# A one-core decoder layer in float32: where the state-space tables, the bias rows, the first far row and the first down weights stand in the queues

## The chip, the cores and the metric

The kernel runs on one core of one Trainium2 chip. The metric is the device time of one execution, in microseconds (us), the median of several runs. "PE" is the matrix engine (TensorE), "DVE" VectorE, "ACT" ScalarE, "POOL" GpSimd, "SP" SyncE, which here does nothing but issue DMAs. ACT and POOL can issue DMAs as well. Every engine works through its own instructions strictly in the order in which they stand in its queue; where one waits, all behind it wait.

## The reference, cut to what matters

One layer, 2048 tokens, width 1024, everything in float32:

```python
h = rms_norm(x, norm1_g); proj = h @ w_in
o_a = swa_sink_mixer(...)        # near attention, window 128, 4 heads
o_b = s5_mixer(...)              # state-space part: A_bar = exp(A*dt), a scan over all tokens, GELU, GLU
o_c = nsa_mixer(...)             # far attention: compressed, selected and window branch, 4 heads
mixed = concat(rms_norm(o_a), rms_norm(o_b), rms_norm(o_c))
x = x + mixed @ w_out
h2 = rms_norm(x, norm2_g)
x = x + relu(h2 @ w_up)**2 @ w_down     # hidden width 4096
```

Both attentions add a bias by distance, looked up in a table `rel_bias` of 32 rows and 8 heads.

## The kernel before

Every float32 product is made of three matmuls on split words (`wh`/`wl`, `hh`/`hl`: the upper bits and the rest), so each operand is cast on ACT (`wh`) and subtracted on DVE (`wl`). The work runs in five stages.

**Front (0 to 153 us here).** The projection is made in tiles of 128 tokens. First the state-space input `u`, then eight tiles `pm_a` of the near heads' columns, then sixteen of `pm_b` and `pm_c`. A tile's product is 24 matmuls into a PSUM bank, of which there are two for `pm`; ACT scales it out of the bank into `po` (L190), squares it into `sq` (L192, one buffer), DVE sums the squares into the last columns of `po` (L193), and POOL stores `po` (L194). A token row's scale `rx` needs the sum of squares of its `x` row. Rows 8 to 15 are loaded in `row_sum`: POOL copies one element of the newest `po_a` sum into the buffer (L118), so that the load, issued by POOL behind it (L119), cannot start earlier; ACT then squares the row (L120). Meanwhile DVE makes the tables of the state-space part (`ssm_tables`): exponentials `rho` of 0 to 16 times the log of the decay, sines and cosines of 11 doubled angles, power tables `k_Ea`/`k_Eb`, and products with the inputs B and C. The bias rows are made in `bias_vectors`: a table `tab` and one-hot matrices `boh` are loaded, PE multiplies them (`bpr`, L797), ACT copies the result to `brv`, POOL stores it (`r`). Their pool "bv" reuses the tables' memory. Weights are loaded into a ring `wraw` (`wr_a`, `wr_b`, `wr_c`) by SP. The order of this stage is a scheduler's: code order with raised priorities (`W_HOIST`).

**Second half of the front, the scan, near attention (153 to 555 us).** Not touched.

**Far attention (555 to 1200 us).** `phase_mix` runs a planner: tasks yield an engine, a cost in ns and a closure, are ranked, and are placed by the planner's own clock; its order is then fixed by hand (`manual_schedule`). The far rows are 16 blocks of 128 tokens. A row loads `tc` (queries, keys, values), POOL scales them (`qdc`, L865), PE turns them (`ptqc`, L872), three branches of logits follow (`pqc`, `pqw`, `pqs`), with their maxima `nmc`, `nmw`, `nms` on DVE; results `ot` are added on POOL into `oc`. A finished row is joined with `oa`, `ob` in `mix`, scaled by row factors (`r_a`, `r_b`, `nr`), turned (`ptx`) and multiplied by `w_out`, whose raw rows `oraw` are split into `wo_h` (ACT) and `wo_l` (DVE, L1491). `early_norms` and `row_norms` make the row factors with a chain of small operations on POOL (L51 to L61). `kBs` holds a mask, loaded as `ohr` and cast (L1412). The GLU of the state-space part (`gpm`, `ga` L767, `ob`) fills PE until about 604 us.

**Up (1200 to 1802 us)** and **Down (1802 us to the end)**: products of 2x2 blocks by seven multiplications, named "1675243" in this order. In Down a chunk `c` of 512 hidden channels needs seven weights `dw`, made from the raw chunk `dr` by differences `dt` on POOL (L2662), a cast on ACT (L2228) and a subtraction on DVE (L2229). Code hoisted by `DOWN_HOIST` places the first chunk's weights among the last instructions of Up, where `e` and `ex` (L2491) free PE's banks `pub`, `puc`. Products "1" and "6" go through `acc…u` on ACT and POOL, the others are added on DVE (`acc`, L2715).

Of the kernel before, what the change touches and what calls it, by code (L numbers as in the profile page):

```python
# [93 lines left out]
def phase_front(tc, C, x, norm1_g, w_in, uT, pd, rh_a, prm, ssm_d, rx_d, consts, extra, later, x_t, r_last, last_bank):  # L94

    nc = tc.nc
    with ExitStack() as ctx:
# [78 lines left out]
        open_, box_x, w_more = {}, [], []  # L176

        def product(t, hs, w, kind, c0, n, part=None):
# [17 lines left out]
            if (kind, t // 8) == ("a", 0):  # L196
                row_sum(t + 8, o[:, n:n + 1])
# [10 lines left out]
        for half in range(2):  # L208
# [25 lines left out]
            with tc.tile_pool(name=f"a_psu{half}", bufs=1, space=PSUM, reuse_waits="tile") as ps_u:  # L234
# [30 lines left out]
                if half == 0:  # L265
# [5 lines left out]
                    gen = ssm_tables(tc, C, S, kp, kf, prm, ssm_d["k"])  # L271
# [85 lines left out]
def ssm_tables(tc, C, S, pool, first, prm, dkp):  # L357
# [22 lines left out]
    with ExitStack() as ctx2:  # L380
        tp2 = ctx2.enter_context(tc.tile_pool(name="si2", bufs=1))
        with ExitStack() as ctx:
# [11 lines left out]
            jt = C["ramp"]  # L394
            xr = tmp([P, 17, G], "xr")
# [12 lines left out]
            sincos(nc, k, sc, th)  # L408

# [38 lines left out]
            yield  # L448
            for dst, top, low in ((C1, c_re, c_im), (C2, c_im, c_re)):
                nc.sync.dma_start(dst[0:64], top)  # L450
                nc.sync.dma_start(dst[64:128], low)
            B1, B2 = (tp2.tile([P, G, 16], F32, name="t_" + n) for n in ("B1", "B2"))
            nc.sync.dma_start(B1[0:64], b_re)
            nc.sync.dma_start(B1[64:128], b_im)
            nc.sync.dma_start(B2[0:64], b_im)
            nc.sync.dma_start(B2[64:128], b_re)
            dT = tp2.tile([16, G], F32, name="t_dT")
            nc.sync.dma_start(dT, d_skip[0].rearrange("(g q) -> q g", q=16))
# [326 lines left out]
def bias_vectors(tc, tp, ps, rel_bias, oh2, ohs, r2, rs):  # L785
# [4 lines left out]
    nc.sync.dma_start(tab[0:32], rel_bias)  # L790
    for src, dst, n in ((oh2, r2, 432), (ohs, rs, 384)):
        for j in range(src.shape[1] // n):
            sl = slice(n * j, n * j + n)
            o = tp.tile([33, 432], F32, tag="b_oh", name=f"boh{n}{j}")
            nc.sync.dma_start(o[:, 0:n], src[:, sl])
            pr = ps.tile([P, 512], F32, tag="pt", name=f"bpr{n}{j}")
            nc.tensor.matmul(pr[0:8, 0:n], tab, o[:, 0:n], start=True, stop=True)  # L797
# [575 lines left out]
def phase_mix(tc, flow, ctx, C, x, gains, B, cmp, w_out, out_norm_g, g2, pd, oa_d, ob, x1, hT, xs, rr, rh, ss_a, ss_b, oc_d, gated_all, release, over, up):  # L1373
# [3 lines left out]
    if True:  # L1377
# [32 lines left out]
        ohr = lp.tile([P, L], F32, tag="sl", name="ohr", bufs=4)  # L1410
        nc.sync.dma_start(ohr[64:96], C["blk"])
        nc.vector.tensor_copy(kBs[64:96], ohr[64:96])  # L1412
# [10 lines left out]
        rows_there, norms_there, most = Event(), Event(), Event()  # L1423
# [42 lines left out]
        def opening():  # L1466
# [87 lines left out]
        def keys(i, tq, twice_k):  # L1554
# [17 lines left out]
            fire(ev["k"], t)  # L1572
# [338 lines left out]
        def finished(i):  # L1911
# [15 lines left out]
            else:  # L1927
                box["oc"] = ev["oc"]
            yield landing(t, 5e5)
            mix = box["mix"]  # L1930
            def rest():
                yield rows_there
                yield norms_there
                for c, r, ns in ((slice(0, 256), late["ra"], 474), (slice(256, 768), late["rb"], 700)):
                    yield "POOL", ns, lambda: nc.gpsimd.tensor_scalar(mix[:, c], mix[:, c], r[:, i:i + 1], 1.0, op0=ALU.mult, op1=ALU.mult)

            def third():
# [5 lines left out]
                yield "POOL", RSQRT_NS, lambda: rsqrt_into(nc, late["sm"], r, ss, 1.0 / 256, 1, "nq", nc.gpsimd)  # L1943
                t = yield "POOL", 474, lambda: nc.gpsimd.tensor_scalar(dst, src, r, 1.0, op0=ALU.mult, op1=ALU.mult)
# [182 lines left out]
        spawn(early_norms(), 60, t0)  # L2127
        spawn(opening(), 60, t0)
# [473 lines left out]
def phase_down(tc, x1, w_down, vd, out):  # L2602
# [8 lines left out]
    with ExitStack() as ctx:  # L2611
# [309 lines left out]
def _shape_constants():  # L2921
# [12 lines left out]
    for off in (29, 30):  # L2934
# [5 lines left out]
        "k_ramp": np.tile(np.arange(T16 + 1, dtype=f), (P, 1)),  # L2940
# [41 lines left out]
```

## Time and profile before

| | |
|---|---|
| median of 3 runs | 2422.76 us (2421.95, 2422.76, 2429.80) |
| the profiled execution | 2422.61 us, its span 2420.8 us, mean granted clock 0.992 |
| PE busy | 2360.3 us, 97% of the span |
| DVE, ACT, POOL busy | 1782.6, 1294.4, 1087.2 us |

PE's row is the one to read: 60.5 us of the span are without a matmul. The profile's list of waits names for each engine and line who ended its idle time, and a table of stretches gives the clock that was granted to PE. A row of the timeline is start, duration, engine, line, operation, result and operands, and in brackets the idle time before it and who ended it.

### The profile page before, as it was taken

To read this page: it belongs to the slowest core of one execution; us is meant where nothing else is said; L and a number is where in the kernel's file an instruction comes from. 1 tells how busy PE (TensorE), PEld (TensorE's weight loads), DVE (VectorE), ACT (ScalarE), POOL (GpSimd) and SP (SyncE) were. 2 spreads that over 40 slices of the span, in tenths; PEclk is the share of its full clock that TensorE was granted. 3 is DMA by queue.
4 is the path that set the end of the run, shared out by engine and by line. 5 is a ranking of instruction groups with operands and counts; after the bars stand their busy time and mean duration, and the time that the engine had idled before them with its cause. 6 is when DMAs were issued, how large, how long until landed. Compare 5 with 4: busy or idle time off the path is not lost. (4 is left out here: it accounts for less than half of the span.)

```text
span 2420.8 us, 37163 instructions
## 1 busy us (share of the span) xinstructions
PE 2360.3 (97%) x12292; PEld 2019.6 (83%) x12292; DVE 1782.6 (74%) x3470; ACT 1294.4 (53%) x2726; POOL 1087.2 (45%) x1210
## 2 busy tenths in 40 slices
PE   8899999999899999999999999999999999999999
PEld 7798999787788889888788888888877888888887
DVE  7866885885877888886855557545567888888886
ACT  5443545775777676665655555544454344433442
POOL 1331122323443454332676665566562554545547
PEclk9899999999999999999999999999999999999999
DMA  8674554641322343112666677655548444344435
GB/s 269 179 253 140 179 157 144 168 151 53 129 75 79 92 120 118 43 56 96 196 205 195 195 217 215 191 158 147 148 145 272 135 130 123 100 138 133 128 102 197
DMA packets 409766, 361.60 MB, mean 149 GB/s; under 512 B 45132, under 2 KB 360290, under 8 KB 407492
## 3 DMA queue, kind: packets, MB, share of 16 engines
q1 hardware_dynamic: 355460, 295.83, 40.5%
q10 hardware_dynamic: 43296, 34.09, 4.5%
q0 software_dynamic: 10816, 29.31, 3.6%
q8 instruction: 97, 1.59, 0.3%
q14 instruction: 97, 0.79, 0.1%
HBM read 236.31 MB, written 128.02 MB: 150 GB/s over the span
## 5 line engine op out<-in xcount | busy, mean ns | idle before, releaser
L2228 ACT CAST v<-vr 128x512 fp32r<-128x512 f32 x224 | 139.4, 624 | 295.7 <-DMA vr<-vd 139.7
L2229 DVE TENSOR_TENSOR v<-vr,v 128x512 fp32r<-128x512 f32 x224 | 237.9, 1071 | 80.2 <-ACT v L2228 79.2
L2392 DVE TENSOR_TENSOR ul<-fs,uh 128x512 fp32r<-128x512 f32 x124 | 112.2, 923 | 104.7 <-ACT uh L2391 104.5
L2694 PE MATMUL pdc<-dw,v 128*128 128x512 f32 x768 | 184.9, 389 | 2.6 <-DVE acc L2715 2.6
L2694 PE MATMUL pda<-dw,v 128*128 128x512 f32 x768 | 184.8, 389 | 0.7 <-ACT acc0u L2700 0.7
L2694 PE MATMUL pdb<-dw,v 128*128 128x512 f32 x768 | 184.8, 389 | 0.0
L2694 PEld LDWEIGHTS pdc<-dw,v 128*128 128x128 f32 x768 | 144.0, 188 | 33.3 <-DVE acc L2715 3.4
L2694 PEld LDWEIGHTS pda<-dw,v 128*128 128x128 f32 x768 | 144.1, 188 | 31.0 <-ACT acc0u L2700 1.1
L2694 PEld LDWEIGHTS pdb<-dw,v 128*128 128x128 f32 x768 | 144.1, 188 | 30.3 <-DVE acc L2715 0.4
L2391 ACT CAST uh<-fs 128x512 fp32r<-128x512 f32 x124 | 74.3, 620 | 160.0 <-POOL fs L2380 123.2
L2392 DVE TENSOR_TENSOR ul<-ur,uh 128x512 fp32r<-128x512 f32 x93 | 87.9, 948 | 68.5 <-ACT uh L2391 68.5
L2539 POOL TENSOR_TENSOR ev<-ex,e 128x512 f32<-128x512 f32 x32 | 43.1, 1347 | 206.7 <-ACT ex L2522 206.7
L1662 ACT CAST ths<-pps 128x512 fp32r<-128x512 f32 (+1 forms) x144 | 79.0, 564 | 72.2 <-PE pps L1646 63.2
L2522 ACT ACTIVATE e<-e 128x512 f32<-128x512 f32 x128 | 81.0, 633 | 53.4 <-DVE e L2491 51.4
L1667 DVE TENSOR_TENSOR tls<-pps,ths 128x512 fp32r<-128x512 f32 (+1 forms) x144 | 92.6, 657 | 23.0 <-ACT ths L1662 22.2
L1997 PE MATMUL pw<-wo_h,mh 128*128 128x512 f32 x256 | 106.6, 416 | 1.2 <-DVE mx L2019 0.9
L2470 PE MATMUL pub<-fh,uh 128*128 128x512 f32 x256 | 101.7, 397 | 4.9 <-DVE e L2491 4.9
L1997 PE MATMUL pw<-wo_h,ml 128*128 128x512 f32 x256 | 104.6, 409 | 0.0
L1997 PE MATMUL pw<-wo_l,mh 128*128 128x512 f32 x256 | 104.2, 407 | 0.0
L2470 PE MATMUL puc<-fl,uh 128*128 128x512 f32 x256 | 99.8, 390 | 1.6 <-DVE fl L2410 1.5
L2470 PE MATMUL pub<-fh,ul 128*128 128x512 f32 x256 | 100.6, 393 | 0.0
L2470 PE MATMUL puc<-fh,ul 128*128 128x512 f32 x256 | 99.8, 390 | 0.7 <-DVE ul L2392 0.7
(581 smaller groups left out, 7604.0 us busy)
## 6 DMA issues: line engine op xcount, KB each, us to landing
vr<-vd SPq DMA_DIRECT2D x224, 256.0 KB
ur<-in_w_up SPq DMA_DIRECT2D x124, 256.0 KB
vd<-ev SPq DMA_DIRECT2D x96, 256.0 KB
vd<-e ACTq DMA_DIRECT2D x64, 256.0 KB
dr<-in_w_down SPq DMA_DIRECT2D x32, 512.0 KB
mx<-in_x ACTq DMA_DIRECT2D x32, 256.0 KB
x<-mx ACTq DMA_DIRECT2D x32, 256.0 KB
vd<-e SPq DMA_DIRECT2D x32, 256.0 KB
```

The costliest lines, as they stand in the source:

```text
L1662: yield "ACT", cast_ns(n), lambda: nc.scalar.copy(th[:, 0:nb], pt[:, 0:nb])
L1667: t = yield "DVE", sub_ns(n), lambda: nc.vector.tensor_tensor(tl[:, 0:nb], pt[:, 0:nb], th[:, 0:nb], op=ALU.subtract)
L1997: t = yield "PE", mm_ns(512), lambda: nc.tensor.matmul(pw[n], a[half][:, j], b[k][:, sl], start=k == 0 and m == 0, stop=k == NK - 1 and m ...
L2228: nc.scalar.copy(dh, src)
L2229: nc.vector.tensor_tensor(dl, src, dh, op=ALU.subtract)
L2391: yield "ACT", 621, lambda: self.nc.scalar.copy(h, src.tile)
L2392: t = yield "DVE", 900, lambda: self.nc.vector.tensor_tensor(l, src.tile, h, op=ALU.subtract)
L2470: nc.tensor.matmul(banks[b], w[:, j], h[:, j], start=k < 4 and j == 0 and i == 0, stop=j == HALF - 1 and i == 2, skip_group_check=True)
L2522: t = yield "ACT", 640, lambda: nc.scalar.activation(r, r, func)
L2539: t = yield "POOL", 1400, lambda: nc.gpsimd.tensor_tensor(E["v" + q].tile, E[x].tile, E[y].tile, op=op)
L2694: nc.tensor.matmul(bank[b, q], x[:, q, j], y[:, j], start=first and j == 0 and n == 0, stop=j == 1 and n == 2, skip_group_check=True)
```

## The change

Four edits in one.

1. **Tables.** The angles are made first; the 17 exponentials are no longer evaluated as one 128x544 polynomial but as one exponential of 128x32 and four doubling products. B, C and D of the tables, `tab` and the one-hot matrices `boh` are loaded by POOL instead of SP; the former wait for the square of row 7, the one-hot matrices have six buffers instead of one.
2. **Weights of `pm_b`.** Each `wr_b` load waits for a POOL copy out of the newest `po_a` sum.
3. **First far rows.** The mask's load and cast become a ranked task (`marks`); the last row's factors (`row_norms`) and the first far row's factors and scalings go to DVE; the loads of `w_out` wait until the first row's `mix` loads are asked for.
4. **Down.** Of the first chunk's weights only "7" and "5" keep a place in the pool that is free early; "2", "4", "3" go to the pool behind it, each with a buffer of its own.

```diff
 def fetch_w(half, kind, c0, n, k, pool, bufs, eng):
     raw = pool.tile([P, n], F32, tag="wraw", ...)
+    if (kind, half) == ("b", 0):
+        nc.gpsimd.tensor_copy(raw[:, 0:1], newest[0])
...
 # product()
     if (kind, t // 8) == ("a", 0):
-        row_sum(t + 8, o[:, n:n + 1])
+        newest[:] = [o[:, n:n + 1]]
+        row_sum(t + 8, newest[0])
...
 # ssm_tables()
-    nc.vector.tensor_tensor(xr, adr.unsqueeze(1).broadcast_to([P, 17, G]), jt.unsqueeze(2)..., op=ALU.mult)
-    rho = exp_acc(nc, tp, xr, [P, 17, G], "e2")
-    nc.vector.tensor_copy(rho16, rho[:, 16])
     for j in range(11):
         nc.vector.tensor_scalar(th[:, j], adi, float(2 ** j), None, op0=ALU.mult)
     sincos(nc, k, sc, th)
+    rho = tmp([P, 17, G], "rho")
+    e = exp_acc(nc, tp, adr, [P, G], "e2")
+    nc.vector.memset(rho[:, 0], 1.0)
+    nc.vector.tensor_copy(rho[:, 1], e)
+    for n in (1, 2, 4, 8):
+        nc.vector.tensor_tensor(rho[:, n + 1:2 * n + 1], rho[:, 1:n + 1], rho[:, n:n + 1].broadcast_to([P, n, G]), op=ALU.mult)
+    nc.vector.tensor_copy(rho16, rho[:, 16])
...
+    for dst in (C1, C2, B1, B2):
+        nc.gpsimd.tensor_copy(dst[:, 0, 0:1], seen)
-    nc.sync.dma_start(dst[0:64], top)
+    nc.gpsimd.dma_start(dst[0:64], top)
...
 # bias_vectors()
-    nc.sync.dma_start(tab[0:32], rel_bias)
+    nc.gpsimd.dma_start(tab[0:32], rel_bias)
-    o = tp.tile([33, 432], F32, tag="b_oh", name=f"boh{n}{j}")
-    nc.sync.dma_start(o[:, 0:n], src[:, sl])
+    o = tp.tile([33, 432], F32, tag="b_oh", name=f"boh{n}{j}", bufs=6)
+    nc.gpsimd.dma_start(o[:, 0:n], src[:, sl])
...
 # phase_mix: far attention
-    ohr = lp.tile([P, L], F32, tag="sl", name="ohr", bufs=4)
-    nc.sync.dma_start(ohr[64:96], C["blk"])
-    nc.vector.tensor_copy(kBs[64:96], ohr[64:96])
+    def marks():
+        yield R["sl"]
+        ohr = lp.tile([P, L], F32, tag="sl", name="ohr", bufs=4)
+        t = yield "SP", 60, lambda: nc.sync.dma_start(ohr[64:96], C["blk"])
+        yield landing(t, 3e5)
+        t = yield "DVE", 1220, lambda: nc.vector.tensor_copy(kBs[64:96], ohr[64:96])
...
 def norms():
     yield most
-    t = yield "POOL", 3300, row_norms
+    t = yield "POOL", 250, lambda: nc.gpsimd.tensor_copy(late["ra"], r_ae)
+    fire(norms_there, t)
+    t = yield "DVE", 1500, row_norms
...
 # finished(i)
+    engine, e = ("POOL", nc.gpsimd) if i else ("DVE", nc.vector)
-    yield "POOL", ns, lambda: nc.gpsimd.tensor_scalar(mix[:, c], mix[:, c], r[:, i:i + 1], ...)
+    yield engine, ns, lambda: e.tensor_scalar(mix[:, c], mix[:, c], r[:, i:i + 1], ...)
...
 # phase_down()
-    for o in ORDER[2:6]:
+    for o in ORDER[2:4]:
         w_high.tile([P, 2, 2, N], F32R, tag="w" + o, name="dw" + o)
+    for o in ORDER[4:]:
+        w_last.tile([P, 2, 2, N], F32R, tag="w" + o, name="dw" + o)
```

The order on the engines moves at three places that matter below (a row is line, operation, result and operands, shape; the changed kernel's lines are numbered some 2 to 25 higher).

ACT in the front, before: from the fourth `wh_b` to the third eviction of `pm_a`; `x_746` is row 8.

```order
L154 ACTIVATE wh_b_3_939<-wr_b_3_936,g_109 128x384
L349 ACT_TABLE_LOAD
L349 ACTIVATE k_sc<-k_sc 128x704
L154 ACTIVATE wh_b_4_1036<-wr_b_4_1033,g_109 128x384
L190 ACTIVATE po_a<-pm_a_716,rx 128x384
L154 ACTIVATE wh_b_5_1043<-wr_b_5_1040,g_109 128x384
L192 ACTIVATE sq_a<-po_a 128x384
L154 ACTIVATE wh_b_6_1085<-wr_b_6_1082,g_109 128x384
L190 ACTIVATE po_a<-pm_a_798,rx 128x384
L192 ACTIVATE sq_a<-po_a 128x384
L120 ACTIVATE x_746,ss<-x_746 128x1024
L190 ACTIVATE po_a<-pm_a_892,rx 128x384
```

The same place now (`x_749` is row 8):

```order
L192 ACTIVATE po_a<-pm_a_719,rx 128x384
L194 ACTIVATE sq_a<-po_a 128x384
L192 ACTIVATE po_a<-pm_a_801,rx 128x384
L194 ACTIVATE sq_a<-po_a 128x384
L120 ACTIVATE x_749,ss<-x_749 128x1024
L192 ACTIVATE po_a<-pm_a_901,rx 128x384
L156 ACTIVATE wh_b_0_877<-wr_b_0_873,g_109 128x384
L156 ACTIVATE wh_b_1_885<-wr_b_1_881,g_109 128x384
L194 ACTIVATE sq_a<-po_a 128x384
L120 ACTIVATE x_832,ss<-x_832 128x1024
L192 ACTIVATE po_a<-pm_a_957,rx 128x384
```

All `wh_b` and the table load have left the stretch ahead of the first two evictions; row 8 still stands ahead of the third, and row 9 with two `wh_b` ahead of the fourth.

DVE from Up to Down, before: `dw…<-dr` and `dw…<-dt` are the weights "7", "5", "2", "4" in this order.

```order
L2491 TENSOR_TENSOR e_20951<-puc_20932,ex_20913 128x512
L2229 TENSOR_TENSOR dw_21152<-dt_21129,dw_21152 128x1024
L2229 TENSOR_TENSOR dw_21160<-dt_21125,dw_21160 128x1024
L2229 TENSOR_TENSOR dw_21168<-dr_21120,dw_21168 128x1024
L2229 TENSOR_TENSOR dw_21173<-dt_21171,dw_21173 128x1024
L2491 TENSOR_TENSOR e_20951<-pub_20952,e_20951 128x512
L2519 TENSOR_TENSOR e_20983<-e_20983 128x512
```

The same place now:

```order
L2514 TENSOR_TENSOR e_20966<-puc_20947,ex_20928 128x512
L2252 TENSOR_TENSOR dw_21168<-dt_21145,dw_21168 128x1024
L2252 TENSOR_TENSOR dw_21176<-dt_21141,dw_21176 128x1024
L2514 TENSOR_TENSOR e_20966<-pub_20967,e_20966 128x512
L2542 TENSOR_TENSOR e_20998<-e_20998 128x512
```

The weights "2" and "4" now stand 10 rows further on, behind six `v` of the first products and right ahead of weight "3"; on ACT their casts moved likewise, behind both `de` and ahead of the copies `acc0u`, `acc1u`.

DVE at about 606 us, shortly before the third far row is turned, before:

```order
L1568 SCALAR_TENSOR_TENSOR kAw<-ptkc_7161,gains,kAw 64x128
L1570 COPY kBw<-kAw 64x128
L1571 COPY kBs<-kAs 64x128
L1720 TENSOR_TENSOR otw_7279<-ptow_7247,ww 128x512
L1598 ISA slw_7257,nmw<-pqw_7259,b_sel 128x384
```

Now the ten steps of `row_norms` (eight of 128x1, then two) stand between `kAw` and `kBw`; the last two of them and what follows:

```order
L1461 TENSOR_SCALAR r_ce<-r_ce 128x16
L1463 TENSOR_TENSOR r_sel<-r_sel,r_ce 128x128
L1588 COPY kBw<-kAw 64x128
L1589 COPY kBs<-kAs 64x128
L1740 TENSOR_TENSOR otw_7269<-ptow_7246,ww 128x512
```

More of the change, by code (lines that the diff above doesn't have):

```diff
@@ L354, with ssm_tables @@
 WEIGHTS_AT = 2
-def ssm_tables(tc, C, S, pool, first, prm, dkp):
+def ssm_tables(tc, C, S, pool, first, prm, dkp, seen):
     nc = tc.nc
@@ L448, in ssm_tables @@
             yield
+            B1, B2 = (tp2.tile([P, G, 16], F32, name="t_" + n) for n in ("B1", "B2"))
+            for dst in (C1, C2, B1, B2):
+                nc.gpsimd.tensor_copy(dst[:, 0, 0:1], seen)
             for dst, top, low in ((C1, c_re, c_im), (C2, c_im, c_re)):
-                nc.sync.dma_start(dst[0:64], top)
[L451 to L456, printed above, removed]
+                nc.gpsimd.dma_start(dst[0:64], top)
+                nc.gpsimd.dma_start(dst[64:128], low)
+            nc.gpsimd.dma_start(B1[0:64], b_re)
+            nc.gpsimd.dma_start(B1[64:128], b_im)
+            nc.gpsimd.dma_start(B2[0:64], b_im)
+            nc.gpsimd.dma_start(B2[64:128], b_re)
             dT = tp2.tile([16, G], F32, name="t_dT")
-            nc.sync.dma_start(dT, d_skip[0].rearrange("(g q) -> q g", q=16))
+            nc.gpsimd.dma_start(dT, d_skip[0].rearrange("(g q) -> q g", q=16))
             zz = tp2.tile([16, 112], F32, name="t_zz")
@@ L1422, in phase_mix @@
         wout = {(k, n): Event() for k in range(NK) for n in range(2)}
-        rows_there, norms_there, most = Event(), Event(), Event()
+        rows_there, norms_there, most, asked, marked = (Event() for _ in range(5))
         pm = kp.tile([P, P], F32, name="pm")
@@ L1472, in opening @@
             fire(opened, t)
+            yield asked
             for n in range(2):
@@ L1475, in opening @@
                 for k in range(NK):
+                    if (k, n) == (2, 0):
+                        later = Event()
+                        fire(later, t + 1500)
+                        yield later
                     yield R["xt"]
@@ L1571, in keys @@
             t = yield "DVE", 300, lambda: nc.vector.tensor_copy(kBs[0:64, ks], kAs[0:64, ks])
-            fire(ev["k"], t)
+            if not i:
+                yield marked
+            fire(ev["k"], max(t, marked.time))
         def values(i):
@@ L1928, in finished @@
                 box["oc"] = ev["oc"]
+                fire(asked, t)
+            engine, e = ("POOL", nc.gpsimd) if i else ("DVE", nc.vector)
             yield landing(t, 5e5)
@@ L1934, in rest @@
                 for c, r, ns in ((slice(0, 256), late["ra"], 474), (slice(256, 768), late["rb"], 700)):
-                    yield "POOL", ns, lambda: nc.gpsimd.tensor_scalar(mix[:, c], mix[:, c], r[:, i:i + 1], 1.0, op0=ALU.mult, op1=ALU.mult)
+                    yield engine, ns, lambda: e.tensor_scalar(mix[:, c], mix[:, c], r[:, i:i + 1], 1.0, op0=ALU.mult, op1=ALU.mult)
             def third():
@@ L2775, in consts @@
             nc.sync.dma_start(C["ident"], k_ident)
-            for n, src in (("ramp", k_ramp), ("forced", k_forced), ("rows31", k_rows31)):
+            for n, src in (("forced", k_forced), ("rows31", k_rows31)):
                 C[n] = cp.tile(list(src.shape), F32, name="c_" + n)
```

35 lines of the change are left out of this document (16 added, 19 removed).

## The prediction, made before the changed kernel was run

> **What bounds the kernel.** I read the page's first part, then the list of waits of PE, then the timeline around each long wait and the table of stretches for the granted clock.
>
> ```profile
> PE 2360.3 (97%) x12292; PEld 2019.6 (83%) x12292; DVE 1782.6 (74%) x3470; ACT 1294.4 (53%) x2726; POOL 1087.2 (45%) x1210
> ...
> PE bpr L797 <- DMA boh<-in_k_oh: 6.6, 2, 5.3
> PE pub L2470 <- DVE e L2491: 4.9, 2, 4.7
> ```
>
> PE is busy all but 60.5 us, and the change takes no matmul away. So it can only shorten PE's waits and the slow clock behind them. A wait row gives total, count and longest: the bias product and the last `pub` lead. All four edits stand beside such a wait, and each is summed where it stands.
>
> **Front: what is lost now.** Rows of the timeline, then the table of stretches (PE, PEld, DVE, ACT, POOL busy; granted clock; DMA).
>
> ```profile
> 61.62 0.61 ACT L154 ACTIVATE wh_b<-wr_b,g 128x384 fp32r<-128x384 f32 x1 [5.84 <-DMA wr_b<-in_w_in]
> 65.36 0.69 PE L83 MATMUL pm_a<-wh_a,hh 128*128 128x384 f32 x1 [3.31 <-ACT po_a L190]
> 67.72 0.19 POOL L118 COPY x<-po_a 128x1 f32<-128x1 f32 x1 [12.09 <-DVE po_a L193]
> 74.32 1.06 ACT L120 ACTIVATE x<-x 128x1024 f32<-128x1024 f32 x1 [5.11 <-DMA x<-in_x]
> 96.06 0.34 SPq L790 DMA_DIRECT2D tab<-in_rel_bias  x1
> 98.69 1.59 PE L797 MATMUL bpr<-boh,tab 33*8 33x432 f32 x2 [5.34 <-DMA boh<-in_k_oh]
> 114.05 0.88 PE L797 MATMUL bpr<-boh,tab 33*8 33x432 f32 x2 [1.27 <-DMA boh<-in_k_oh]
> 153.27 0.53 PE L83 MATMUL pm_c<-wh_c,hh 128*128 128x396 f32 x1
> ```
> ```profile
> 66.00:67.00 1.00, 1.00 (x5) 1.00 (x4) 0.97 (x5) 1.00 (x3) 0.00 (x0) 0.50 0.10 24
> 71.00:72.00 1.00, 1.00 (x7) 1.00 (x6) 0.96 (x3) 0.00 (x0) 0.48 (x1) 0.99 0.77 223
> 104.00:105.00 1.00, 1.00 (x5) 0.88 (x3) 1.00 (x3) 0.00 (x0) 1.00 (x1) 0.50 0.59 218
> 116.00:117.00 1.00, 1.00 (x5) 1.00 (x4) 0.88 (x5) 0.00 (x0) 0.39 (x1) 0.50 0.39 134
> ```
>
> ACT stands 5.84 on a weight of `pm_b`, the eviction behind it comes late, PE waits 3.31, and the clock is 0.50 until about 71. The one-hot loads cost 5.34 and 1.27, each with a slow stretch behind it. At half clock half of the time is lost: of the slow stretches, 65.4 to 71.1, 98.7 to 105.1 and 115.3 to 118.6 (read off the same table, of which the first and last rows of each kind stand above), 2.8, 3.2 and 1.65. With the waits, 9.92, that is 17.5 us.
>
> *What the change removes.* The `wh_b` casts leave ACT's queue ahead of those evictions: the 3.31 goes. The exponentials shrink:
>
> ```profile
> L321 DVE TENSOR_TENSOR e2t<-e2p,e2r 128x544 f32<-128x544 f32 x6 | 4.4, 726 | 0.2
> L322 DVE TENSOR_SCALAR e2p<-e2t 128x544 f32<-128x544 f32 x6 | 2.6, 441 | 0.1
> L316 DVE SCALAR_TENSOR_TENSOR e2r<-e2k,e2xc 128x544 f32<-128x544 f32 x1 | 0.7, 726 | 0.0
> ...
> L326 DVE TENSOR_SCALAR e2t<-t_xr 128x544 f32<-128x544 f32 x1 | 0.4, 434 | 0.0
> ...
> L155 DVE SCALAR_TENSOR_TENSOR wl_b<-wr_b,g,wh_b 128x384 fp32r<-128x384 f32 x8 | 4.9, 615 | 0.1
> L193 DVE TENSOR_REDUCE po_a<-sq_a 128x6 f32<-128x384 f32 x6 | 3.3, 549 | 2.1 <-ACT sq_a L192 2.1
> ```
>
> Twelve rows take 7.0, eleven more of 0.43 to 0.73 sum to 6.8. The 23 small ones that replace them cost about 0.19 each (the smallest rows of DVE, 0.17, stand below), 4.4, and the doublings 1.1: 8.3 saved. The eight `wl_b` (4.9), four sums (2.2) and some 3.6 of DVE's idle time leave the stretch too, so the table's memory is free about 19 earlier: `tab` is asked for near 77 instead of 96, the one-hots land near 83 to 84.
>
> *What it adds.* Row 8's load still waits for the sum of the first `po_a` (67.72 above). DVE, still in order, reaches that sum near 66.8, one earlier than now; the square of row 8 then runs near 72.5 instead of 74.32, and it stands ahead of the third eviction. PE, no longer stalled for the third tile, is ready for the fifth at 70.45 and waits until 74.2: 3.8 plus 2.8 slow. So the 3.31 comes back two tiles later. The bias products now stand between the fifth and seventh tiles (81 to 93), three tiles earlier, and catch their data later than PE wants it: 2.3, and 1.5 slow; one `brv` buffer makes them wait for each other, 1.1; row sums that now stand behind DVE's table, 2.7. After: 3.8+2.8+2.3+1.5+1.1+2.7 = 14.2 against 17.5, −3.3. Walking the new order instance by instance with these durations, PE reaches the first `pm_c` at 145.4 to 148.9 where it now stands at 153.27; some of the row sums' cost then still lies ahead, and from this view I get −4.4. I take **−5**, a little beyond both, since the 2.7 is the least certain of the new waits. Its ends are −10 (half of the 14.2 absent) and +3 (the table no earlier than 90, so that the bias products cost 6.6 and 4.85 slow as now, in place of 2.3, 1.5 and 1.1). POOL's new loads and copies are costed at nothing: POOL stood idle for 12.09 before 67.72 and works on small things there; what it costs if that cover is gone is rival C. The `wr_b` gate itself makes no one wait: `pm_b` is wanted after eight tiles of `pm_a`, and eight casts of 0.61 fit between their evictions.
>
> **Mask gate at 558.**
>
> ```profile
> 559.25 1.22 DVE L1412 CAST kBs<-ohr 32x2048 fp32r<-32x2048 f32 x1 [5.34 <-DMA ohr<-in_k_blk]
> 559.25 1.30 POOL L59 TENSOR_TENSOR r_t<-r_t,r_h 128x16 f32<-128x16 f32 x1
> 561.33 0.47 PE L83 MATMUL gpm<-glu_h,zh 128*128 128x512 f32 x1 [2.26 <-DVE ga L767]
> 562.72 1.68 POOL L865 TENSOR_TENSOR qdc<-tc,rh_c 128x512 f32<-128x512 f32 x2
> 563.87 1.11 PE L872 MATMUL ptqc<-c_ident,qdc 128*128 128x128 f32 x4 [0.52 <-POOL qdc L865]
> 564.00:565.00 1.00, 1.00 (x5) 1.00 (x6) 0.00 (x0) 0.00 (x0) 0.39 (x1) 0.50 0.01 4
> ```
>
> Without the cast `ga` comes early and the 2.26 goes. But PE's next need, `qdc`, stands on POOL behind a chain of tiny operations that ends at 562.7 with or without the cast (one of them took 1.30 beside it). PE then waits there: **−0.5**, ends −2.8 (both waits gone) and 0. The cast's 1.22 moves behind `ga`, and the first reader of the mask, the selected branch, comes later than that; its 5.34 of idle time shows that DVE has room.
>
> **Far opening near 606.**
>
> ```profile
> 605.02 1.82 SPq L1478 DMA_DIRECT2D oraw<-in_w_out  x4
> 607.88 0.38 SPq L1517 DMA_DIRECT2D tc<-pb  x1
> 612.79 2.60 POOL L865 TENSOR_TENSOR qdc<-tc,rh_c 128x512 f32<-128x512 f32 x2 [1.70 <-DMA tc<-pb]
> 614.41 1.12 PE L872 MATMUL ptqc<-c_ident,qdc 128*128 128x128 f32 x4 [3.60 <-POOL qdc L865]
> 117.01 0.17 DVE L60 TENSOR_SCALAR rqt<-rqt 128x8 f32<-128x8 f32 x1
> ```
>
> PE's 3.60 ends with a load, `tc`, that SP issues behind four `oraw`. Now two `mix` loads go first, of which one waits until `ob` is stored; `oraw` and `tc` follow. So `tc` is no earlier: the edit relieves POOL, which wasn't last. DVE gets ten factor steps of about 0.2 ahead of `kBw`, 2.1 us, and eight steps and three scalings, 2.5 us, ahead of the first row's next softmax, where it is nearly full. The two blocks together, 4.6, delay what DVE feeds to PE (`kBw`, then the split exponentials); my walk of the new order puts PE 3 later by 625. POOL gives up the same steps, in its own slower form, and a queue that is shorter there brings later `qdc` earlier. I take **+1**: the walk, less 2 for that. Ends: −3 (`tc` lands earlier, most of the 3.60 gone) and +5 (both DVE blocks in full).
>
> **Down.**
>
> ```profile
> 1787.70 4.40 DVE L2229 TENSOR_TENSOR dw<-dt,dw 128x1024 fp32r<-128x1024 f32 x2
> 1792.02 3.37 DVE L2229 TENSOR_TENSOR dw<-dr,dw 128x1024 fp32r<-128x1024 f32 x1
> 1796.56 0.68 DVE L2491 TENSOR_TENSOR e<-pub,e 128x512 f32<-128x512 f32 x1
> 1797.30 0.80 PE L2470 MATMUL pub<-fh,uh 128*128 128x512 f32 x1 [4.72 <-DVE e L2491]
> 1801.56 1.65 ACT L2228 CAST v<-vr 128x512 fp32r<-128x512 f32 x3
> 1813.91 3.02 PE L2694 MATMUL pda<-dw,v 128*128 128x512 f32 x12 [0.71 <-ACT acc0u L2700]
> 1819.00 1.66 PE L2694 MATMUL pdc<-dw,v 128*128 128x512 f32 x6 [2.07 <-DVE acc L2715]
> ```
>
> Weights "2" and "4" hold DVE from 1792.02 to 1796.56, in front of the `e` that frees PE's bank. They move 10 rows on, so `e` runs at about 1792.0: 4.5 earlier, and with it the 4.72 goes and the slow clock behind (1797.3 to 1801.3, 2.0). Now 4.72+2.0+0.71+2.07 = 9.5 are lost up to "4". But who is late next? PE wants the first `v` near 1798.2, and their casts on ACT (1801.56 now) come 3.4 earlier only: 1.3. `acc0u`, which empties a bank, now stands on ACT behind the casts of "2", "4" and "3", each of 1.1 by the row of `v` (three of half the size take 1.65): PE finds it 2.3 late. The sums `acc`, 4.5 earlier, are still 1.7 late, since PE comes earlier too. That is 5.3 of new waits: 9.5 − 5.3 = 4.2. Read the other way, the row at 1819.00 ends with DVE's `acc`, whose chain starts at `e` and moves by 4.5. I take **−4.5**; ends −7 (half of the new waits) and −1.5 (half as much again).
>
> **Sum.** −5 −0.5 +1 −4.5 = −9 on the profiled 2422.61 (span 2420.8 and 1.8 around it, equal to the median 2422.76 within 0.2): 2413.6. All low ends together make −23, all high ends +6.5. A change under 0.3%, 7.3 us, can hardly be told from none.
>
> [...] The clock was 0.50 at 564, after waits of 2.26 and 0.52, and at 116 after 1.27. [...]
>
> ```profile
> x<-in_x POOLq DMA_DIRECT2D x8, 512.0 KB, 4.7
> ```
>
> POOL's loads of `x` rows landed 4.7 after issue with DVE nearly full. [...]
>
> **Rivals.** *A, every wait named goes and none comes:* −17.5 −2.8 −7 = −27.3, 2395. For it: all of them have one releaser, which the change moves. Against: row 8's load and `qdc` keep theirs. 0.07. *B, the gains are given back:* the front gains 2, the far opening costs 4, Down gains 4: 2420.6, no change that can be told. For it: DVE at 0.93 to 1.00 in every stretch where it gets work. 0.34. *C, slower:* POOL's queue becomes the chain of the front. It now holds `tab`, which waits for DVE's table, six one-hot loads, `wr_b` copies and the stores of `r`, which wait on ACT, and all of them stand ahead of the loads of rows 11 to 15. A square that comes late costs PE what the late eviction costs at 65.36, 3.31 and 2.8 slow, 6.1. Three such rows more make −9 + 18.3 = +9: 2432. For it: POOL's row at 67.72 shows that a wait on DVE holds all its loads. Against: that idle 12.09 is room as well. It decides from the third row on, and then `pm_c` starts after 160. 0.06. *D, short waits leave the clock at full:* the 2.8 and 1.5 of the front don't come, 2409. 0.05. The forecast, 2407 to 2415, has 0.48. Faster is forecast, A and D, 0.60; same 0.34; slower 0.06. The range, 2403 to 2423, leaves out A and C and holds B.
>
> **What would show it.** Right: no wait for `po_a` at 65, one of 3 to 4 near 70 to 74 with row 8's square ahead of the eviction; `tab` issued near 77; `pm_c` starting 145 to 149; `qdc` as PE's releaser near 563 and still near 614; no wait of `pub` at 1792, and small ones for `v`, `acc0u`, `acc`. Wrong: `tab` later than 85, row squares of ACT waiting over 5 for POOL loads, PE waiting for DVE near 607, or the far rows shifted by a chain that I followed only to 625.

## The result: slower by 0.9%, and the profile after

| | before | changed |
|---|---|---|
| median | 2426.27 us (2421.95 to 2429.8) | 2447.2 us (2445.64 to 2449.3) |
| ratio | | 1.0088, 95% interval 1.0064 to 1.0111 |
| profiled span | 2420.8 | 2443.8 |

The time lies above the range, and the kernel got slower where faster was forecast. The page's first row and PE's list of waits of the changed kernel:

```profile
PE 2367.5 (97%) x12292; PEld 2025.1 (83%) x12292; DVE 1779.6 (73%) x3496; ACT 1298.0 (53%) x2726; POOL 1085.6 (44%) x1217
```
```profile
PE pk L535 <- DVE oCA L528: 12.6, 2, 7.4
...
PE bpr L804 <- issue: 5.7, 1, 5.7
PE ptqc L879 <- POOL qdc L872: 5.3, 4, 3.1
PE pdc L2719 <- DVE acc L2740: 5.0, 3, 2.3
PE pv L635 <- DVE U L622: 3.7, 1, 3.7
PE pm_a L83 <- ACT po_a L192: 2.6, 1, 2.6
...
PE ptr L1475 <- DVE r_sel L1463: 2.0, 1, 2.0
```

`pub` has left the head of the list, as the down edit wants. At the top stands `pk`, the product with `oCA`, which did not appear before; `pv`, in a stage that no edit touches, rose from 1.4 to 3.7.

PE runs the same 12292 matmuls in both, so the same matmul can be looked up in both traces, and the difference of its starts read as a shift. Taken as the median over 12 us, PE is later than in the first profile by these amounts (us):

| at (us, before) | 80 | 125 | 160 | 270 | 400 | 598 | 625 | 740 | 1210 | 1780 | 2000 | 2400 |
|---|---|---|---|---|---|---|---|---|---|---|---|---|
| changed | -2.0 | 3.7 | 13.1 | 17.7 | 17.3 | 18.1 | 23.1 | 23.8 | 23.8 | 24.1 | 22.9 | 23.0 |

Front +13.1, start of the scan +4.2 (160 to 400), far rows +5.7 (598 to 1210), Down -1.2 (1780 to 2000); the end, 23.0, is the difference of the spans. The timeline of the front, where most of it is lost:

```profile
71.02 1.06 ACT L120 ACTIVATE x<-x 128x1024 f32<-128x1024 f32 x1 [4.60 <-DMA x<-in_x]
72.69 0.44 PE L83 MATMUL pm_a<-wh_a,hh 128*128 128x384 f32 x1 [2.63 <-ACT po_a L192]
75.46 0.53 POOL L797 DMA_DIRECT2D tab<-in_rel_bias  x1 [2.32 <-DVE t_v L497]
84.41 3.04 PE L804 MATMUL bpr<-boh,tab 33*8 33x432 f32 x4 [5.68 <-issue]
108.51 0.54 POOL L119 DMA_DIRECT2D x<-in_x  x1
117.78 1.06 ACT L120 ACTIVATE x<-x 128x1024 f32<-128x1024 f32 x1 [7.27 <-DMA x<-in_x]
118.36 0.73 DVE L526 TENSOR_TENSOR oCA<-k_AR,k_C 128x544 f32<-128x544 f32 x1 [8.00 <-DMA pa<-po_a]
120.73 2.08 PE L535 MATMUL pk<-oCA,k_Y 128*128 128x256 f32 x4 [7.37 <-DVE oCA L528]
136.45 0.73 DVE L526 TENSOR_TENSOR oCA<-k_AR,k_C 128x544 f32<-128x544 f32 x1 [5.58 <-DMA dca<-oCA]
```

Up to 80 us the rows are those of the forecast: row 8's square now holds the third eviction, PE waits 2.63 for it, and `tab` is asked for at 75.46. Then they leave it. PE waits 5.68 for the bias products (2.3 forecast) and stands for `pk`, 7.37 and later 5.26, on a DVE that itself stands idle for 8.00 and 5.58. Two of the prediction's own signs of being wrong are there: a row's square that waits over 5 for its load (7.27), and PE waiting for DVE in the far opening (`r_sel`, 2.00).

### The profile page after: what moved, and what is told of

Read it like the earlier page. It is cut to its first block, busy times and chain, and to the rows that moved or that the text cites. A ratio compares the mean times of both kernels' runs of the same rounds, so it can differ in the third digit from the quotient of the medians.

```text
span 2443.8 us, 37223 instructions
## 1 busy us (share of the span) xinstructions
PE 2367.5 (97%) x12292; PEld 2025.1 (83%) x12292; DVE 1779.6 (73%) x3496; ACT 1298.0 (53%) x2726; POOL 1085.6 (44%) x1217
## 4 chain that ended last, share of the span: by engine, by line
PE 55%; issue 5%; POOL 4%; DVE 4%; DMA 2%; ACT 2%; ACTq 0%; SPq 0%; POOLq 0%; DVEq 0%
PE pdc L2719 7%; PE pdb L2719 7%; PE pda L2719 7%; PE pw L2019 7%; PE pua L2493 4%; PE puc L2493 4%; PE pub L2493 4%; PE pdd L2719 3%; PE pos L1699 2%; PE pps L1666 2%; PE pud L2493 2%; POOL ev L2562 2%; POOL fs L2403 2%; DMA vd<-e 1%; ACT e L2545 1%
## 5 line engine op out<-in xcount | busy, mean ns | idle before, releaser
L2252 DVE TENSOR_TENSOR v<-vr,v 128x512 fp32r<-128x512 f32 x224 | 243.3, 1095 | 76.1 <-ACT v L2251 75.9
L1687 DVE TENSOR_TENSOR tls<-pps,ths 128x512 fp32r<-128x512 f32 (+1 forms) x144 | 93.3, 658 | 18.9 <-ACT ths L1682 17.3
L2493 PE MATMUL puc<-fh,uh 128*128 128x512 f32 x256 | 100.1, 391 | 0.0
L2493 PE MATMUL pua<-fh,uh 128*128 128x512 f32 x256 | 99.7, 390 | 0.0
```

Source lines behind the costliest of these rows:

```text
L1687: t = yield "DVE", sub_ns(n), lambda: nc.vector.tensor_tensor(tl[:, 0:nb], pt[:, 0:nb], th[:, 0:nb], op=ALU.subtract)
L2252: nc.vector.tensor_tensor(dl, src, dh, op=ALU.subtract)
L2493: nc.tensor.matmul(banks[b], w[:, j], h[:, j], start=k < 4 and j == 0 and i == 0, stop=j == HALF - 1 and i == 2, skip_group_check=True)
```

## The experiments

The numbers of the first four columns are PE's shift gained in each stage against the first profile, in one profiled execution each, and the ratio of times to the kernel before.

| kernel | front (to 160) | scan (160 to 400) | far (598 to 1210) | Down (1780 to 2000) | ratio (95%) |
|---|---|---|---|---|---|
| before, again | -2.7 | 0.9 | -1.4 | 3.0 | |
| changed | 13.1 | 4.2 | 5.7 | -1.2 | 1.0088 (1.0064 to 1.0111) |
| changed, one one-hot buffer | 2.4 | 2.6 | 5.4 | -1.7 | 1.0034 (1.0020 to 1.0048) |
| changed, bias rows on SP, one buffer | 5.0 | 4.8 | 3.3 | 0.3 | 1.0045 (1.0030 to 1.0061) |
| changed, `brv` placed first | 14.5 | 4.3 | 4.5 | -0.5 | 1.0081 (1.0064 to 1.0098) |
| changed, no gate, one buffer | 8.1 | 2.8 | 3.8 | 0.5 | 1.0065 (1.0052 to 1.0078) |
| changed, B, C, D on SP, one buffer | 0.6 | 2.4 | 6.6 | -2.1 | 1.0034 (1.0021 to 1.0048) |
| far edits alone | -2.4 | 3.2 | 3.3 | 3.6 | 1.0018 (1.0006 to 1.0029) |
| far, row factors on POOL | -1.8 | 1.1 | 8.0 | 1.2 | 1.0039 (1.0025 to 1.0053) |
| far, no gate on `w_out` | 1.0 | 0.1 | 7.4 | 2.5 | 1.0034 (1.0022 to 1.0046) |
| far, first row on POOL | 2.4 | 0.2 | 3.0 | 3.7 | 1.0015 (1.0003 to 1.0027) |
| mask task alone | -2.9 | 0.6 | -1.2 | 2.7 | 1.0004 (0.9993 to 1.0014) |
| down edit alone | -1.1 | 0.8 | 0.0 | -1.8 | 0.9984 (0.9974 to 0.9993) |
| down edit alone, again | 0.5 | 0.7 | -1.0 | -0.2 | 0.9987 (0.9978 to 0.9996) |
| tables and down | 2.8 | 0.8 | -2.1 | -0.8 | 1.0002 (0.9993 to 1.0010) |
| gate, tables and down | 8.6 | 0.1 | -0.6 | -1.4 | 1.0024 (1.0015 to 1.0034) |
| gate and down | 4.5 | 0.9 | | | 0.9989 (0.9980 to 0.9998) |

(Of the last one's profile only the first 600 us can be compared.) Rows whose front is unedited scatter by -2.9 to +2.4 there, so a single profile tells a stage to some 3 us; the ratios tell the whole better.

**The kernel before, again.** The same file once more.

> The kernel before, profiled once more. Theory: where a wait makes the slow clock start differs from run to run, so its waits agree with the first profile within 1 us in each stage, its slow clock differs by multiples of 3.4 us, and the shift at the end is between 0 and +6. Rival: the profile shown was an ordinary one; the shift is within 0.5 everywhere.

It took 2422.2 us. The stages moved by -2.7 to +3.0 with no edit, and the sum by -0.4: the theory holds for the slow clock, which came at other places (10.2 us in Down instead of 6.8), but not for the waits, which agree within 2 us per stage and not within 1, nor for the sum.

**One one-hot buffer.**

```diff
-    o = tp.tile([33, 432], F32, tag="b_oh", name=f"boh{n}{j}", bufs=6)
+    o = tp.tile([33, 432], F32, tag="b_oh", name=f"boh{n}{j}")
```

> The changed kernel with one buffer for the one-hot matrices instead of six (POOL still loads them). Theory 'memory': with six buffers the rows brv lie where the pool of oCA begins, so DVE's first oCA waits for the last store of the bias rows (8.0 us idle in the profile of the changed kernel, PE's pk 7.4). Then that wait and the slow clock behind it are gone here: pk at most 1 us for the first oCA, PE's shift against the kernel before at 160 us falls from +13.1 to 0 to +4, time near 2437. Rival 'queue': pk waits because everything of POOL's queue (one-hot loads, row loads, stores) comes late; then some other wait of 5 to 8 us takes its place, shift at 160 us stays above +9, time above 2443.

2433.36 us against 2447.2: 1.0034 instead of 1.0088. The front falls from +13.1 to +2.4, and DVE's 8.00 before the first `oCA` is gone. So the six buffers cost some 11 to 13 us, more than half of the whole loss. But the expectation's reason had a second reading, since this edit also changes the order: DVE now has its first two `oCA` between the third and the fourth sum of `po_a` and the third behind the fourth, where the changed kernel has all of them behind the eighth.

**`brv` placed first.** All edits and six buffers; only addresses differ.

```diff
+    tp.tile([8, 432], F32, tag="b_rv", name="brv_first")
     tab = tp.tile([33, 8], F32, tag="b_tab", name="tab")
```

> The changed kernel with all its edits and its six one-hot buffers, but the buffer brv is placed in front of them in the pool. The order of instructions is the same on every engine; only addresses differ: the first oCA now lies over one-hot buffers, not over brv. Theory 'memory': the first oCA no longer waits for the last store of the bias rows, pk's 7.4 us go with 0 to 3.4 us of slow clock, shift at 160 us falls from +13.1 to +3 to +6, time near 2438. Rival (the late queue, not the address, makes pk wait): no change, +13, time 2445 or more.

The wait did go, and nothing was gained (1.0081). DVE, ACT and PE of this kernel:

```profile
112.94 0.72 DVE L526 TENSOR_TENSOR oCA<-k_AR,k_C 128x544 f32<-128x544 f32 x1
...
120.06 1.06 ACT L120 ACTIVATE x<-x 128x1024 f32<-128x1024 f32 x1 [6.46 <-DMA x<-in_x]
...
121.60 0.42 DVE L195 TENSOR_REDUCE po_b<-sq_b 128x4 f32<-128x256 f32 x1 [7.31 <-issue]
...
122.71 2.08 PE L535 MATMUL pk<-oCA,k_Y 128*128 128x256 f32 x4 [6.26 <-DVE oCA L528]
```

The first step of `oCA` runs at 112.94 without idle time, so the store of `brv` no longer holds it. Its last step (L528) stands on DVE behind a sum of `po_b`; that waits 7.31 for a square which on ACT stands behind the square of a token row, and ACT stands 6.46 for that row's load. So the theory "the wait for the stores" falls as the cause of the time: it and the late row end within a microsecond of each other in the changed kernel (118.36 and 117.78 above), and the row alone is enough to hold PE. What the six buffers do comes earlier, in the order: with them `oCA` lies over the pool of the bias rows, its first instruction waits for that pool's last transfers (for stores of `brv`, or here for one-hot loads), and the scheduler puts it behind them; there it falls into the wait for row loads. With one buffer it waits for none of them and stands early. That the dependence is what made the scheduler choose the place is read from the orders of the three kernels.

**Bias rows on SP; no gate; B, C and D on SP.** Each is the changed kernel with one one-hot buffer and one more piece undone: `tab` and `boh` back on SP; the POOL copy ahead of `wr_b` taken out; B, C and D back on SP without their wait.

```diff
 # bias rows on SP
-    nc.gpsimd.dma_start(tab[0:32], rel_bias)
+    nc.sync.dma_start(tab[0:32], rel_bias)
-    nc.gpsimd.dma_start(o[:, 0:n], src[:, sl])
+    nc.sync.dma_start(o[:, 0:n], src[:, sl])
 # no gate
-    nc.gpsimd.tensor_copy(raw[:, 0:1], newest[0])
 # B, C, D on SP
-    for dst in (C1, C2, B1, B2):
-        nc.gpsimd.tensor_copy(dst[:, 0, 0:1], seen)
-    nc.gpsimd.dma_start(dst[0:64], top)
+    nc.sync.dma_start(dst[0:64], top)
...
```

> The changed kernel with the table and the one-hot matrices loaded by SP again, one buffer: the whole third block of the first edit undone. 'Memory' alone: like the run with one buffer, within 3 us. 'Queue' (the loads behind POOL's row copies and weight copies make the bias products late): another 4 to 6 us faster than with one buffer on POOL, shift at 160 us -3 or lower, time near 2432.

> The changed kernel with one one-hot buffer and without the gate on the weights of pm_b. With the gate and one buffer the shift was +2.4 at 160 us, with 7.0 us of ACT idle for row 14's load. If the gate is to blame for the late row loads (its copies and SP's loads behind it), the shift falls to -1 to -4; if the order of ACT is (row 14's square ahead of the work for pk), it stays +1 to +4.

> The changed kernel with one one-hot buffer and B, C, D loaded by SP without a wait, as before. If POOL's loads of B, C, D are why the four stores of uT leave 3.25 us after the first uo instead of 0.98, they leave at 0.98 here, and the shift does not grow by 2.9 between 235 and 270 us. If it is the gate or the one-hot loads, it stays 3.25. Front otherwise as with one buffer, +1 to +4 at 160 us.

On SP the bias rows gain nothing (1.0045 against 1.0034, intervals overlap), so the "queue" rival falls: POOL's load of `tab` and `boh` is not what is slow. (The median is 4.9 us above that with one buffer, outside the 3 of the 'memory' reading too.) Without the gate the kernel is slower (1.0065), against both expected signs; with all else changed the gate helps, by some 7 us. With B, C and D on SP the time is that of one buffer. The stretch that no edit touches does respond. POOL and DVE of the changed kernel:

```profile
252.49 2.98 POOL L176 DMA_DIRECT2D uT<-uo  x4 [22.86 <-DVE Bp L578]
...
262.10 0.42 DVE L622 TENSOR_TENSOR U<-U,rxu 128x256 f32<-128x256 f32 x1 [5.31 <-DMA U<-uT]
```

The first `uo` of this stretch starts at 249.23, and its store leaves POOL 3.26 later. In the five kernels with B, C and D on POOL this distance is 3.10 to 3.26; in every other profile, the one with all edits but these loads included, it is 0.98. There the third store comes late instead, so its first `U` still comes 11.96 after the first `uo` (12.4 to 13.0 with the loads on POOL, 10.1 to 11.1 with the other fronts). This accounts for some 2 us of the 4.2; for the rest, the slow clock of 6.83 at 261.3 is the likely one. The row names as releaser DVE's `Bp`, the first operation behind the four `uo`; why the store waits for that one is open. The run with B, C and D on SP loses 2.4 in this stage as well, so their loads are not shown to be what costs the time.

**Tables and down; gate, tables and down; gate and down.** The kernel before with parts of the first half added: only the arithmetic of the tables (angles first, doublings), only the gate, or both, each with the down edit. The lines are those of the change:

```diff
 # tables
+    e = exp_acc(nc, tp, adr, [P, G], "e2")
...
 # gate
+    nc.gpsimd.tensor_copy(raw[:, 0:1], newest[0])
 # down, in all three
-    for o in ORDER[2:6]:
+    for o in ORDER[2:4]:
...
```

> The kernel before with the tables' arithmetic alone (angles first, doubling products; no load moved, no gate) and the down weights' edit. The raw weights of pm_b stand on ACT as before, oCA0 to oCA2 stand early on DVE as with one one-hot buffer. Theory: the front's loss came from the gates and the six buffers, not from the arithmetic, so PE's shift at 160 us is -1 to -5, Down gives another 2, and the time is 3 to 7 us below the kernel before's. Rival: any earlier bias product meets PE before its data, as with all edits; the shift at 160 us is +1 to +4 and the time the same as the kernel before's within 2.

> As the last, with the tables' arithmetic too; bias rows, B and C loaded by SP, one one-hot buffer. If earlier tables gain once the gate has cleared ACT, the shift at 160 us is below that of the last; if the early bias products meet PE before their data, it is 2 to 5 us above it.

> The kernel before with the gate on the weights of pm_b and the down edit, nothing else. po_a's 3.31 us wait at 65 us goes (no cast of wh_b ahead of the first two evictions). If the gate is good by itself, shift at 160 us -2 to -5 and the time 4 to 8 us below the kernel before's; if row 8's square takes its place, the front gives 0 and the time is 2 to 4 us below.

Against the down edit alone (0.9984, 0.9987) the gate costs nothing that the times can tell (0.9989; its one profile has the front at +4.5), the tables some 4 us (1.0002; the intervals just meet), both together some 9 (1.0024). Earlier tables lose time by themselves: the rival of the first expectation holds in its numbers, and so does the second reading of the next one (a front of 8.6, 4.1 above that of gate and down). PE of the kernel with tables and down:

```profile
65.31 0.69 PE L83 MATMUL pm_a<-wh_a,hh 128*128 128x384 f32 x1 [4.54 <-ACT po_a L190]
84.72 0.88 PE L799 MATMUL bpr<-boh,tab 33*8 33x432 f32 x2 [3.39 <-DMA boh<-in_k_oh]
98.39 0.89 PE L799 MATMUL bpr<-boh,tab 33*8 33x432 f32 x2 [0.75 <-DMA boh<-in_k_oh]
108.22 0.80 PE L799 MATMUL bpr<-boh,tab 33*8 33x384 f32 x2 [2.14 <-ACT wh_c L154]
...
140.22 1.13 PE L530 MATMUL pk<-oCA,k_Y 128*128 128x256 f32 x4 [2.05 <-ACT kst L534]
```

The bias wait fell from 6.6 to 4.1, so the bias products themselves are not where the time goes; the waits for `pk` are. From 119 us to the end of this stage PE waits for nothing else in any profile: 3.9 to 12.6 us in seven of the eight kernels with earlier tables, and not at all in the eighth (B, C and D on SP, whose front, +0.6, is the least of the eight) or in the kernels with the tables of before.

In the traces the waits for `pk` lead back to late transfers, of a token row or of a store (`x` and `dca` in the brackets of the front's timeline). Earlier bias rows bring their copies `r2w` earlier as well, four of 1080 KB each, issued by SP. The first one in the kernel before, then in the changed one:

```profile
126.00 0.52 SPq L806 DMA_DIRECT2D r2w<-r  x1
```
```profile
108.22 0.53 SPq L813 DMA_DIRECT2D r2w<-r  x1
```

With earlier tables it is issued at 103 to 115 us, with those of before at 123 to 129, behind the last row load. The ten row loads that POOL issued less than 1 us ahead of it or later took 7.9 to 9.8 us to land, all others in these profiles 4.0 to 7.3. In the changed kernel row 14's load was issued 7.1 later than in the kernel before and took 9.19 instead of 5.08; the last store of `brv`, issued behind it, took 9.02. In the kernel with the least front all row loads had left before `r2w`. That these copies are what slows the loads and stores is read from the profiles; no run holds them back.

**Far edits alone, and three with one piece undone.** All far edits of the change, put into the kernel before:

```diff
+        spawn(marks(), 40, t0)
+    t = yield "DVE", 1500, row_norms
+    yield asked
+    engine, e = ("POOL", nc.gpsimd) if i else ("DVE", nc.vector)
...
```

> The kernel before with the far rows' edits alone (mask task, factors on DVE, w_out gate). Theory: the loss of 5.7 us between 600 and 1200 us in the profile of the changed kernel belongs to these edits, so PE's shift is 0 within 0.5 until 600 us and +4 to +7 at 1200, time slower by 4 to 7. Rival: the far loss came with the late front (the stage met other transfers); then the shift at 1200 is -2 to +2 and the time is the same within 2.

1.0018, some 4.4 us: the loss belongs to these edits, with a front that is not late (+3.3 in the profile, +0.9 to +6.4 between 598 and 625, then 2 given back). The undone pieces:

```diff
 # row factors on POOL
-    t = yield "POOL", 250, lambda: nc.gpsimd.tensor_copy(late["ra"], r_ae)
-    fire(norms_there, t)
-    t = yield "DVE", 1500, row_norms
+    t = yield "POOL", 3300, row_norms
 # no gate on w_out
-    yield asked
 # first row on POOL
-    engine, e = ("POOL", nc.gpsimd) if i else ("DVE", nc.vector)
+    engine, e = "POOL", nc.gpsimd
```

> The kernel before with the far edits, but the last row's factors (row_norms) stay on POOL, ahead of the copy of r_a. With all far edits PE's shift goes from +0.9 at 598 us to +6.4 at 625 and 4.1 at 740. If row_norms on DVE is the cost (2.0 us wait of ptr for r_sel, kBw behind it), the rise is at most 2 here and the time near the kernel before's. If not, it is still +4 to +6.

> The kernel before with the far edits, but the loads of w_out don't wait for the first row's mix loads. If that gate is the cost (tc late behind it), the rise between 598 and 625 us is at most 2. If DVE's new work is, it is still +4 to +6.

> The kernel before with the far edits, but the first row's factors and scalings stay on POOL. If these 2.5 us of DVE are the cost, the rise between 598 and 650 us is at most 2. If row_norms or the gate is, it is still +4 to +6.

None of them removes the loss: the rise from 598 to 625 is 4.0, 6.4 and 4.4, two are no faster (1.0039, 1.0034, intervals that overlap that of all far edits), the third leaves the time as it is (1.0015). PE's longer waits with all far edits alone, then with the row factors on POOL:

```profile
610.23 0.39 PE L1468 MATMUL ptr<-r_sel 128*128 128x16 f32 x2 [2.00 <-DVE r_sel L1456]
616.59 1.12 PE L872 MATMUL ptqc<-c_ident,qdc 128*128 128x128 f32 x4 [1.92 <-POOL qdc L865]
620.57 0.39 PE L1634 MATMUL pqc<-kcA,qA 128*128 128x24 f32 x1 [1.78 <-DVE nmc L1611]
622.88 0.80 PE L1692 MATMUL pow<-tlw,vw 128*128 128x256 f32 x2 [1.28 <-DVE tlw L1680]
633.33 0.38 PE L1692 MATMUL pow<-thw,vw 128*128 128x256 f32 x1 [2.69 <-ACT thw L1675]
```
```profile
613.77 0.66 PE L872 MATMUL ptqc<-c_ident,qdc 128*128 128x128 f32 x4 [2.87 <-POOL qdc L865]
617.23 0.79 PE L1692 MATMUL pow<-thw,vw 128*128 128x256 f32 x2 [2.80 <-ACT thw L1675]
...
631.89 1.11 PE L1728 MATMUL ptoc<-c_ident,oTc 128*128 128x128 f32 x4 [3.10 <-DVE ml L1978]
```

The wait for `r_sel` (2.00) is the one forecast, and it is gone in the second kernel; 2.80 for ACT's `thw` and 3.10 for DVE's `ml` stand in its place. The fixed order of this stage comes from a planner, and each edit gives another order with other waits of 1 to 3 us.

**The mask task alone.** Of the far edits only this:

```diff
-        nc.sync.dma_start(ohr[64:96], C["blk"])
-        nc.vector.tensor_copy(kBs[64:96], ohr[64:96])
+        spawn(marks(), 40, t0)
...
```

> The kernel before with the mask task alone of the far edits. Undoing one of the three others left +4 to +6 between 598 and 625 us each time. If each of the three costs by itself, the mask alone costs nothing: shift within 1 of the front's all the way to 1200 us. If the planner's new order around the mask task is the cost, the rise is still +4.

1.0004, shift -1.2 over the far rows: the mask alone costs nothing. That each of the three others costs by itself is not shown, since undoing any one of them gained nothing. PE waits 3.28 for `qdc` where it waited 2.26 for `ga` and 0.52 for `qdc`.

**The down edit alone**, run twice.

```diff
-        for o in ORDER[2:6]:
+        for o in ORDER[2:4]:
             w_high.tile([P, 2, 2, N], F32R, tag="w" + o, name="dw" + o)
+        for o in ORDER[4:]:
+            w_last.tile([P, 2, 2, N], F32R, tag="w" + o, name="dw" + o)
```

> The kernel before with the down weights' edit alone. Theory: e is freed early but the bank copies acc0u and the sums acc are late instead, as in the profile of the changed kernel, so the gain is 1 to 1.5 us, all between 1790 and 1850 us. Rival, the prediction's own term: 4.5 us.

> The kernel before with the down edit alone, once more: 2 us of waits less in Down by the first profile, so 1 to 4 us below the kernel before's; rival, the 3.9 us of the first timing were chance and it is the same.

0.9984 and 0.9987: 3 to 4 us faster, clear of 1 both times; more than the 1 to 1.5 expected, less than the prediction's 4.5. PE of the first:

```profile
1809.27 4.27 PE L2696 MATMUL pda<-dw,v 128*128 128x512 f32 x12 [1.92 <-ACT acc0u L2702]
1814.67 1.64 PE L2696 MATMUL pdc<-dw,v 128*128 128x512 f32 x6 [1.13 <-DVE acc L2717]
1817.81 1.65 PE L2696 MATMUL pdc<-dw,v 128*128 128x512 f32 x6 [1.26 <-DVE acc L2717]
```

From 1780 to 2000 us the ten profiles with this edit (the changed kernel and its variants among them) shift by -2.1 to +0.5, mean -0.9; the seven without it, the first one counted as 0, by 0 to +3.7, mean 2.4. The difference, 3.3, agrees with the times. The -1.2 of the first comparison was small because the profile before happened to be the quickest of its seven there. This kernel beats the kernel before and the changed one, the former by 0.15% only.

## Why the prediction was wrong

- **Front, -5 forecast, +13.1 measured.** The step that failed is the sum of new waits, 14.2. Its first entries came: row 8's load, square and eviction came back as a wait of 2.63 (3.8 forecast), and the table's end at 75.46 (77). But at its last entry, "row sums that now stand behind DVE's table, 2.7", the runs showed 12.6, for `pk`: with six one-hot buffers `oCA` stands behind the bias rows' work, and at that place ACT waits 7.27 for a row and DVE 8.00. The six buffers have no term in the sum, and that was the largest mistake; one run with one buffer took back 10.7 of the 13.1. The new order of DVE was read for what stood there, not for what it then depended on.
- **"`tab` is asked for near 77 instead of 96", as a gain.** The time was right (96.06 to 75.46) and the sign wrong. The tables alone, with the old loads, made the kernel some 4 us slower than without, though the bias products waited less. What came instead is the waits for `pk`, which the sum did not have, behind rows and stores that landed late beside the earlier copies of the bias rows.
- **Nothing in the scan.** It was left out of the sum, since no line of it changed. It lost 4.2, of which some 2 go with the stores of `uo` that POOL holds and the rest probably with slow clock.
- **Mask gate, -0.5.** Right in kind, too small to be told in size: the shift is 18.1 at 555 and at 598, and from 555 to 598 it moves by -0.7 with the mask task alone. PE waits 3.05 for `qdc` instead of 2.26 for `ga` and 0.52 for `qdc`, as forecast. The view only names another releaser.
- **Far opening, +1 (-3 to +5).** Mechanism right, size wrong: +5.7 here, 1.0018 alone (4.4 us). `tc` indeed came no earlier, and the 2.00 for `r_sel` stood where forecast. The step that failed is "the walk, less 2 for that", the 2 for a shorter queue on POOL: POOL still waited for `tc` before this `qdc`, 2.72 instead of 1.70, so nothing came earlier by it. The walk's 3 by 625 was too low as well: the shift had grown by 5.0 there, though PE's waits between 598 and this place sum to 8.5, against 8.1 before. The rest lies under a slow stretch of 17.07 us (626.6 in the list below), for which the forecast has no term. How much of the loss is due to that stays open: gate, tables and down has a stretch as long at this place and lost nothing in the far rows (-0.6).
- **Down, -4.5.** Right in mechanism and nearly in size: 3.3 by the stages, 3.0 to 3.9 by the times of the edit alone. `acc0u` (1.75 in the changed kernel, 2.3 forecast) and `acc` (2.27 and 1.98, 1.7 forecast) are the next late ones; the wait for the first `v`, 1.3 forecast, was 0.39.
- **Rivals.** C came true in its sign and its test (`pm_c` starts at 166.38, the limit was 160), at 0.06 far too low. Its mechanism came only in part: rows 14 and 15 were late in part because their loads took longer to land (9.19 and 9.46 us), and moving the bias loads off POOL gained nothing. D falls for the front, as shown below. The chance of 0.60 for faster had little support: all four terms were small differences of sums of waits, each with an error as large as itself.

## What to carry to other kernels

More buffers in a short-lived pool need not be free when a later pool lies over it: here the scheduler moved the later work behind them, and the wait showed far from the edit (`pk`, 12.6 us). So compare the place of the first user of that memory, before and after. An operand that is ready earlier need not gain: with the tables alone earlier, the bias wait fell from 6.6 to 4.1 us and the kernel still lost some 4, so look at where its consumer stands in the queue and what that place waits for. It also releases earlier what waits for it (here `r2w`, issued at 108.22 instead of 126.00), so look at which transfers then meet. Where a stage is tuned to waits of 1 to 3 us, time each edit of a bundle alone: here one of four paid by itself.

## What the runs showed of the hardware

In two profiles the granted clock is 1.00 or 0.50 and nothing between, and the stretches at 0.50 last 3.41 us or a multiple of it. All of them but the last, which the end of the kernel cuts (start, length in us):

```
before   64.2 6.83 | 98.3 6.83 | 115.4 3.41 | 562.5 3.41 | 613.7 3.41 | 624.0 6.83 | 1794.8 6.83
changed  73.6 3.41 | 83.8 6.83 | 118.0 6.83 | 138.5 6.83 | 261.3 6.83 | 582.2 3.41 | 626.6 17.07 | 650.5 6.83
```

In the kernel before, of matmuls in a row, one of 128x384 starts 0.174 us after the other at 1.00 and 0.320 at 0.50, one of 128x512 0.227 and 0.427 (medians): a stretch at 0.50 loses 46 or 47% of its time, a little less than the half that the prediction takes.

A wait of 2.63 at 70 us in the changed kernel was followed by such a stretch, and so was one of 1.27 at 113 in the kernel before, so rival D falls for the front; but the waits of 1.75, 2.27 and 1.98 in Down of the changed kernel got none, and similar ones in the run of the down edit alone got 3.41. So the length of a wait did not tell here whether a slow stretch followed. The kernel before has 17.1 us of slow clock in its front in one profile and 10.2 in the other. This is probably one source of the scatter of some 3 us per stage.

POOL's eight loads of `x` rows landed 4.7 us after issue in the kernel before, 5.4 in the changed one (medians). With one one-hot buffer the ratio is 1.0034 where POOL loads the bias rows too and 1.0045 where SP does: no cost of loading them by POOL shows.
